# Thirty-five seeded shifts of a planner's priorities and engine preferences, two transformer blocks on one core

## The chip, the cores and the metric

One Trainium2 chip, one of its cores. The metric is the device time of one execution in microseconds (us), here the median of three runs. Each of the core's engines runs its own queue in order: TensorE (PE in the profile), VectorE (DVE), ScalarE (ACT), GpSimd (POOL) and SyncE (SP), the last of which here only issues transfers.

## The reference

A row block of 256 tokens of width 1024 goes through two blocks of two layers each. The first block has adaptive norms (shift, scale and gate from a condition vector), a mixer and a squared-ReLU FFN in each layer; the mixers are a chunked relative-position attention with 16 heads and a gated MLP. The second block has two layers of mixed attention. Everything is float32.

```python
def first_block(x, c, ...):
    cond = jax.nn.silu(c)
    for i in range(DEPTH):
        mod = cond @ ada_w[i] + ada_b[i]
        sh1, sc1, g1, sh2, sc2, g2 = [t[:, None, :] for t in jnp.split(mod, 6, axis=-1)]
        h = rms_norm(x, norm_mix[i]) * (1.0 + sc1) + sh1
        y = chunked_relpos_attention(h, ...) if i == 0 else chunked_spatial_gating(h, ...)
        x = x + g1 * y
        h = rms_norm(x, norm_ffn[i]) * (1.0 + sc2) + sh2
        x = x + g2 * squared_relu_mlp(h, ffn_w1[i], ffn_w2[i])
    return x

def reference(...):
    x = first_block(x, c, ada_w, ada_b, ...)
    return second_block(x, rel_bias_2, pre_norm_g_2, w_in_2, ...)
```

The places that matter here are the entry of the first attention (the projection of `h` to q, k and v), its scores, softmax and out-projection, and the entry of the first FFN.

## The kernel before

The kernel is a program generator. It first records operations (`Op`) in the order of the mathematics, each with its buffers, its dependencies and its alternatives of engine, and then a planner puts them into one order, which is emitted as it stands: each engine executes its instructions in that order. Nothing is reordered on the chip.

**Data.** Tokens lie on partitions in two halves (`t` = 0 and 1). All large weights come from HBM in one list (`wall`), in groups of 1 MB that each hold two tiles of 128x1024, through a ring of four slots named `raw` (`load_group`, issued by SP at L860; a slot is free again when the last reader of both its tiles is done). A weight tile is split into two reduced-precision float32 parts that together carry the precision: `hi` by a cast on ACT (L899) and `lo` by a subtraction on DVE (L903). A product is then a triple of matmuls on PE (L800, L801, L802: hi by hi, hi by lo, lo by hi), with activations split in the same way (L1006 on ACT, L1008 on DVE). Scores and other small products are single matmuls (L788) and transposes are L828. `arena` and `arena_r` are SBUF, `banks` the eight PSUM banks.

**The stretch around the change.** Attention opens with eight steps `k`, each with a weight tile for q and k and one for v, its share of the activations scaled and split, and eight triples. Heads then run in pairs: scores (L788), bias and row minimum (L766 on DVE, 128x256 and 128x128), exponential (L713 on ACT), three transposes of the probabilities (L828) into a PSUM bank, the copy of that bank to SBUF (L728 on ACT, 128x384), and three matmuls with v (L788, 128x64). The scores, the transposes and the results each have a set of banks. The out-projection (weights `ao`) has eight weight tiles and four accumulators. The rows of the condition vector's product (`adc`, L766 on DVE, 128x1024, and `adg`, L758) read their weights from the same ring and are needed for the shift and scale of later norms. After the out-projection come the residual (L739), the sum of squares (L951 on DVE or L949 on ACT), the scaling by the norm (L986 on DVE or L988 on ACT), the transposes, the shift and scale (`affine`, L1064 on DVE or L1070 on ACT, four pieces of 128x128) and the split, and then the first FFN's triples. Its first eight hidden blocks are computed with tokens on partitions and go through a copy (L1359 in `ffn`, executed by the helper at L728 on ACT or L731 on DVE) and four transposes.

**What sets the order.** `Sched.schedule` (L408) plays the program through several times with durations of its own (`round`), derives a due time for each operation and keeps the due times of the best round as priorities `pri`. A last `round` with these priorities gives the order: among the operations that could start about now on an engine, it takes the one with the lowest `pri`. For an operation that may run on ACT or DVE it takes the engine on which start plus duration is least, with 0.6 us added for DVE unless the operation is marked critical:

```python
s, _, e = min(((start_of(o, a[0]), a[1] + (0.0 if o.crit else self.EXTRA.get(a[0], 0.0)), a[0]) for a in o.alts),
        key=lambda x: x[0] + x[1])
```

`shift` can add noise to the priorities of a stretch, but the list of its seeds, `SHIFTS`, is empty.

## Time and profile before

| | |
|---|---|
| time, median of 3 runs | 987.65 us (987.05 to 988.52) |
| the profiled execution's own time | 988.6 us |
| its span | 986.5 us |
| PE busy | 963.1 us (98% of the span) |
| DVE busy | 766.9 us (78%) |
| ACT busy | 616.0 us (62%) |
| HBM read | 214.48 MB, 218 GB/s over the span |

The span is the time from the first to the last instruction; 2.1 us of the execution's own time lie around it. Busy is the time in which an engine executes, waits excluded. The profile lists for each engine what it waited for (the waits), gives the busy time of every engine in chosen stretches together with PEclk, the share of TensorE's full clock of 2.4 GHz that was granted (half of it is 1.2 GHz), and shows single instructions with their start and duration (the timeline). Consecutive instructions of an engine overlap by some 0.1 us in the timeline, so that starts, not durations, show what a sequence costs.

### The profile page before, as it was taken

To read this page: it belongs to the slowest core of one execution; us is meant where nothing else is said; L and a number is where in the kernel's file an instruction comes from. 1 tells how busy PE (TensorE), PEld (TensorE's weight loads), DVE (VectorE), ACT (ScalarE), POOL (GpSimd) and SP (SyncE) were. 2 spreads that over 40 slices of the span, in tenths; PEclk is the share of its full clock that TensorE was granted. 3 is DMA by queue.
4 is the path that set the end of the run, shared out by engine and by line. 5 is a ranking of instruction groups with operands and counts; after the bars stand their busy time and mean duration, and the time that the engine had idled before them with its cause. 6 is when DMAs were issued, how large, how long until landed. Compare 5 with 4: busy or idle time off the path is not lost.

```text
span 986.5 us, 14776 instructions
## 1 busy us (share of the span) xinstructions
PE 963.1 (98%) x5652; PEld 844.5 (86%) x5652; DVE 766.9 (78%) x1300; ACT 616.0 (62%) x1119; POOL 17.2 (2%) x38
## 2 busy tenths in 40 slices
PE   6999899999999999999999999999999999999997
PEld 5878588899998888999999889999889888898986
DVE  6889999978767975987767876765679778898783
ACT  6589857555455666844445764544657689776892
POOL 1000000000100000000000000010000001000000
PEclk7999899999999999999999999999999999999999
DMA  9977676778876594766654375676635126361311
GB/s 348 350 294 293 234 324 255 268 287 306 300 288 235 191 384 171 299 222 239 220 198 146 129 256 217 239 259 224 220 150 211 53 108 228 118 233 68 107 62 44
DMA packets 32087, 216.47 MB, mean 219 GB/s; under 512 B 3793, under 2 KB 4049, under 8 KB 7185
## 3 DMA queue, kind: packets, MB, share of 16 engines
q1 hardware_dynamic: 30816, 211.98, 57.6%
q0 software_dynamic: 1200, 3.56, 1.2%
q8 instruction: 44, 0.72, 0.3%
q14 instruction: 27, 0.21, 0.1%
HBM read 214.48 MB, written 1.05 MB: 218 GB/s over the span
## 4 chain that ended last, share of the span: by engine, by line
PE 87%; ACT 5%; DVE 4%; DMA 2%; issue 1%; SPq 0%; DVEq 0%; ACTq 0%
PE banks L800 26%; PE banks L802 26%; PE banks L801 26%; PE banks L788 4%; PE banks L828 3%; ACT arena L713 2%; DMA raw<-in_wall 1%; ACT arena_r L899 1%; DVE arena L739 1%; ACT arena L728 1%; PE banks L814 1%; PE banks L815 1%; DVE arena L766 1%; DVE arena_r L903 1%; DMA arena<-in_xin 1%
## 5 line engine op out<-in xcount | busy, mean ns | idle before, releaser
L800 PE MATMUL banks<-arena_r 128*128 128x512 f32 (+1 forms) x1568 | 544.1, 347 | 1.3 <-ACT arena_r L1006 0.9
L801 PE MATMUL banks<-arena_r 128*128 128x512 f32 (+1 forms) x1568 | 534.6, 341 | 0.9 <-DVE arena_r L903 0.8
L802 PE MATMUL banks<-arena_r 128*128 128x512 f32 (+1 forms) x1568 | 534.0, 341 | 0.0
L903 DVE TENSOR_TENSOR arena_r<-raw,arena_r 128x1024 fp32r<-128x1024 f32 x300 | 359.7, 1220 | 47.1 <-ACT arena_r L899 46.2
L899 ACT CAST arena_r<-raw 128x1024 fp32r<-128x1024 f32 x300 | 305.7, 1044 | 40.5 <-DMA raw<-in_wall 19.4
L802 PEld LDWEIGHTS banks<-arena_r 128*128 128x128 f32 x1568 | 297.8, 190 | 34.2 <-DVE arena_r L1008 0.2
L800 PEld LDWEIGHTS banks<-arena_r 128*128 128x128 f32 x1568 | 298.3, 190 | 32.0 <-ACT arena_r L1006 1.3
L801 PEld LDWEIGHTS banks<-arena_r 128*128 128x128 f32 x1568 | 298.5, 190 | 31.6 <-DVE arena_r L903 2.1
L713 ACT ACTIVATE arena<-banks 128x256 f32<-128x256 f32 (+1 forms) x100 | 44.0, 443 | 143.9 <-PE banks L802 140.5
L713 ACT ACTIVATE arena<-arena 128x256 f32<-128x256 f32 (+10 forms) x160 | 66.7, 422 | 46.7 <-DVE arena L951 23.0
L1006 ACT ACTIVATE arena_r<-arena 128x256 fp32r<-128x256 f32 (+1 forms) x116 | 54.9, 485 | 63.7 <-DVE arena L758 35.5
L766 DVE CUSTOM_DVE_ANT_0 arena<-raw,arena 128x1024 f32<-128x1024 f32 x64 | 82.0, 1281 | 13.0 <-DMA raw<-in_wall 12.4
L758 DVE SCALAR_TENSOR_TENSOR arena<-banks,arena 128x256 f32<-128x256 f32 (+1 forms) x80 | 37.2, 466 | 51.9 <-ACT arena L713 36.8
L1008 DVE SCALAR_TENSOR_TENSOR arena_r<-arena,arena_r 128x256 fp32r<-128x256 f32 (+1 forms) x116 | 57.4, 504 | 22.8 <-ACT arena_r L1006 22.1
L788 PE MATMUL banks<-arena 128*128 128x64 f32 (+3 forms) x432 | 68.3, 295 | 3.8 <-DMA arena<-in_ident 3.5
L828 PE MATMUL banks<-arena 128*128 128x128 f32 x372 | 58.9, 286 | 11.3 <-ACT arena L728 4.5
L788 PEld LDWEIGHTS banks<-arena 128*128 128x128 f32 x432 | 58.9, 197 | 12.4 <-ACT arena L713 3.7
L828 PEld LDWEIGHTS banks<-arena 128*128 128x128 f32 x372 | 46.7, 148 | 22.8 <-ACT arena L728 6.0
L728 ACT COPY arena<-banks 128x512 f32<-128x512 f32 (+3 forms) x106 | 50.8, 495 | 18.4 <-PE banks L802 9.0
L739 DVE TENSOR_TENSOR arena<-arena 128x512 f32<-128x512 f32 (+6 forms) x128 | 51.6, 431 | 5.0 <-ACT arena L713 1.8
L758 DVE SCALAR_TENSOR_TENSOR arena<-raw,arena 128x1024 f32<-128x1024 f32 x32 | 40.9, 1279 | 5.0 <-DMA raw<-in_wall 4.8
L739 DVE TENSOR_TENSOR arena<-banks,arena 128x512 f32<-128x512 f32 (+1 forms) x48 | 30.0, 641 | 18.0 <-PE banks L802 11.2
(44 smaller groups left out, 381.6 us busy)
## 6 DMA issues: line engine op xcount, KB each, us to landing
raw<-in_wall SPq DMA_DIRECT2D x194, 1024.0 KB, 4.9
raw<-in_wall SPq DMA_DIRECT2D x8, 512.0 KB, 9.1
arena<-in_nbias SPq DMA_DIRECT2D x4, 512.0 KB, 7.3
arena<-in_rows POOLq DMA_DIRECT2D x3, 512.0 KB, 6.6
arena<-in_xin SPq DMA_DIRECT2D x2, 512.0 KB, 4.7
out_dram<-arena SPq DMA_DIRECT2D x4, 256.0 KB, 2.0
arena<-in_dbias POOLq DMA_DIRECT2D x2, 384.0 KB, 3.6
arena<-in_wsT POOLq DMA_DIRECT2D x1, 512.0 KB, 4.6
```

Source lines behind the costliest of these rows:

```text
L713: nc.scalar.activation(out=res(out), in_=res(in_), func=func, scale=res(scale), **kw, **({"accum_out": res(accum)} if accum is not None el ...
L728: alts = [("ACT", (0.05 if psum else 0.093) + n / 1200.0, lambda: nc.scalar.copy(out=res(out), in_=res(in_)))]
L739: alt = ("DVE", 0.068 + n / 960.0, lambda: nc.vector.tensor_tensor(out=res(out), in0=res(a), in1=res(b), op=op))
L758: return self.S.op(("DVE", dur, lambda: nc.vector.scalar_tensor_tensor(out=res(out), in0=res(a), scalar=res(s), in1=res(b), op0=op0, op1=o ...
L766: return self.S.op(("DVE", dur, lambda: nc.vector.tensor_tensor_reduce(out=res(junk if out is None else out), in0=res(a), in1=res(b), scal ...
L788: o = self.S.op(("PE", max(n, 96) * 0.00167, lambda: nc.tensor.matmul(res(out), lhsT=res(l), rhs=res(r), start=start, stop=stop)), rd, [ou ...
L800: nc.tensor.matmul(o, lhsT=lh, rhs=rh, start=start, stop=False)
L801: nc.tensor.matmul(o, lhsT=lh, rhs=rl, start=False, stop=False)
L802: nc.tensor.matmul(o, lhsT=ll, rhs=rh, start=False, stop=stop)
L828: nc.tensor.transpose(res(o), res(i), res(ident))
L899: alts = [("ACT", 0.093 + D / 1200.0, lambda: nc.scalar.copy(out=res(hi), in_=res(src))), ("DVE", 0.068 + D / 1920.0, lambda: nc.vector.te ...
L903: dve = ("DVE", 0.068 + D / 960.0, lambda: nc.vector.tensor_tensor(out=res(lo), in0=res(src), in1=res(hi.f32()), op=ALU.subtract))
```

## The change

The list of seeds gets 35 entries. Each of them picks a stretch of due times, adds normal noise to the priorities of some of the operations there, and now also to a number of each operation, `lean`, that takes the place of the fixed 0.6 us which was added for DVE. The computation, the operations and their dependencies stay the same; what changes is the order on the engines and, for operations with two alternatives, the engine.

```diff
--- before.py
+++ after.py
@@ -314,7 +314,7 @@
 
 
 class Op:
-    __slots__ = ("alts", "pri", "deps", "users", "ndep", "bufs", "table", "ready", "fin", "eng", "extra", "kind", "cnt", "seq", "cyc", "need", "crit", "start", "alt", "tab", "rows")
+    __slots__ = ("alts", "pri", "deps", "users", "ndep", "bufs", "table", "ready", "fin", "eng", "extra", "kind", "cnt", "seq", "cyc", "need", "crit", "start", "alt", "tab", "rows", "lean")
 
 
 LAT_SAME = {"PE": 0.0, "ACT": 0.13, "DVE": 0.13, "POOL": 0.15, "SP": 0.0}
@@ -337,8 +337,10 @@
     HOLD = {"ACT": 0.5, "DVE": 0.5}
     RUSH = 2.0
     WARM = 3300
-    EXTRA = {"DVE": 0.6}
-    SHIFTS = ()
+    SHIFTS = (90566615, 56086312, 43099052, 89024882, 76868707, 18636298, 90523558, 93111676, 38614557,
...
 
     def __init__(self):
         self.ops = []
@@ -358,6 +360,7 @@
         o.users = []
         o.cnt, o.crit = 1, self.crit
         o.cyc, o.rows = (0, 1.0), 128
+        o.lean = 0.0 if self.crit else 0.6
         o.ready, o.fin, o.eng = 0.0, None, None
         deps = set()
         bufs = []
@@ -427,24 +430,29 @@
                 due[o] = t
             for o in self.ops:
                 o.pri = due[o] - (self.RUSH if o.crit else 0.0)
-        pri = list(best[1])
+        order = list(zip(best[1], (o.lean for o in self.ops)))
         for seed in self.SHIFTS:
-            self.shift(best[1], pri, seed)
-        for o, o.pri in zip(self.ops, pri):
+            self.shift(best[1], order, seed)
+        for o, (o.pri, o.lean) in zip(self.ops, order):
             pass
         out = self.round(spaces, slots)
         return [(o, alt, tab, [b.off for b in o.bufs]) for o, alt, tab in out]
 
     @staticmethod
-    def shift(base, pri, seed):
+    def shift(base, order, seed):
 
         rng = np.random.default_rng(seed)
         lo, hi = min(base), max(base)
-        mid, width = rng.uniform(lo, hi), rng.choice([8.0, 20.0, 60.0])
-        size, share = rng.choice([0.7, 2.0, 5.0]), rng.choice([0.1, 0.4, 1.0])
+        mid, width = lo + rng.random() * (hi - lo), rng.choice([6.0, 15.0, 40.0])
+        size, share, turn = rng.choice([0.7, 2.0, 6.0]), rng.choice([0.05, 0.3, 1.0]), rng.choice([0.0, 0.1, 0.5])
         for i, b in enumerate(base):
-            if abs(b - mid) < width and rng.random() < share:
-                pri[i] += size * rng.standard_normal()
+            if abs(b - mid) < width:
+                p, q = order[i]
+                if rng.random() < share:
+                    p += size * rng.standard_normal()
+                if rng.random() < turn:
+                    q += rng.standard_normal()
+                order[i] = p, q
 
     def round(self, spaces, slots):
         for o in self.ops:
@@ -558,7 +566,7 @@
                         _, s, i = min(wait)
                         o = cand[i][1]
                 if len(o.alts) > 1:
-                    s, _, e = min(((start_of(o, a[0]), a[1] + (0.0 if o.crit else self.EXTRA.get(a[0], 0.0)), a[0]) for a in o.alts),
+                    s, _, e = min(((start_of(o, a[0]), a[1] + (o.lean if a[0] == "DVE" else 0.0), a[0]) for a in o.alts),
                             key=lambda x: x[0] + x[1])
                 if best is None or s < best[0]:
                     best = (s, o, e)
```

The order of SP, which issues the loads, stays as it was. 17 operations change their engine, of them 9 at the end of the attention and the entry of the first FFN: two sums of squares go from DVE to ACT, one half of a norm's scaling goes from ACT to DVE and the other back, three shift-and-scale operations change places (two to DVE, one to ACT), and two copies of 128x512 (L1359) go to DVE. Line numbers of the changed kernel are 8 higher (L713 is L721, L899 is L907 and so on).

On PE the order is unchanged up to about 25 us, changed between 25 and 225 us, and nearly unchanged after that. Three places follow; a row is an instruction's line, operation, output, inputs and shape, with xN for N in a row.

ACT towards the end of the scores, before; L713 with inputs in `arena` is the exponential, L899 the cast of an out-projection weight, and the 128x384 copy is that of the transposed probabilities:

```order
L899 CAST arena_r<-raw 128x1024
L713 ACTIVATE arena<-arena 128x256
L713 ACTIVATE arena<-arena 128x128
L713 ACTIVATE arena<-arena 128x256
L899 CAST arena_r<-raw 128x1024
L713 ACTIVATE arena<-arena 128x128
L713 ACTIVATE arena<-arena 128x256
L713 ACTIVATE arena<-arena 128x128
L713 ACTIVATE arena<-arena 128x256
L899 CAST arena_r<-raw 128x1024
L713 ACTIVATE arena<-arena 128x128
L728 COPY arena<-banks 128x384
```

and the changed kernel there:

```order
L736 COPY arena<-banks 128x512
L736 COPY arena<-banks 64x256
L721 ACTIVATE arena<-arena 128x128
L736 COPY arena<-banks 64x256
L736 COPY arena<-banks 128x384
L736 COPY arena<-banks 128x512
L907 CAST arena_r<-raw 128x1024
L736 COPY arena<-banks 128x384
L721 ACTIVATE arena<-arena 128x128
L736 COPY arena<-banks 128x384
L721 ACTIVATE arena<-arena 128x256 x2
L907 CAST arena_r<-raw 128x1024
```

In the first the copy comes behind three casts and eight exponentials; in the second one such copy stands ahead of the first cast and two more ahead of the second.

PE at the same place, before; 128x512 of L788 are scores, L828 transposes, 128x64 the products with v, and L800 to L802 here triples of the out-projection:

```order
L788 MATMUL banks<-arena 128x512
L788 MATMUL banks<-arena 128x256
L800 MATMUL banks<-arena_r 128x512
L801 MATMUL banks<-arena_r 128x512
L802 MATMUL banks<-arena_r 128x512
L800 MATMUL banks<-arena_r 128x512
L801 MATMUL banks<-arena_r 128x512
L802 MATMUL banks<-arena_r 128x512
L828 MATMUL banks<-arena 128x128 x3
L788 MATMUL banks<-arena 128x64
L828 MATMUL banks<-arena 128x128 x9
```

and the changed kernel there:

```order
L796 MATMUL banks<-arena 128x256 x2
L836 MATMUL banks<-arena 128x128 x6
L796 MATMUL banks<-arena 128x512
L796 MATMUL banks<-arena 128x64 x3
L836 MATMUL banks<-arena 128x128 x3
L796 MATMUL banks<-arena 128x64 x6
L808 MATMUL banks<-arena_r 128x512
L809 MATMUL banks<-arena_r 128x512
L810 MATMUL banks<-arena_r 128x512
```

The products with v of three heads now stand ahead of the first out-projection triples, where there was one product behind two triples.

DVE around the last weight of the out-projection and the entry of the first FFN, before; L903 is a weight's second part (first row the out-projection's last, the others the FFN's), L739 the residual, L951 the sum of squares:

```order
L903 TENSOR_TENSOR arena_r<-raw,arena_r 128x1024
L758 SCALAR_TENSOR_TENSOR arena<-arena 128x1
L739 TENSOR_TENSOR arena<-banks,arena 128x512
L739 TENSOR_TENSOR arena<-arena 128x512
L951 ISA arena<-arena 128x512
L951 ISA arena 128x1
L739 TENSOR_TENSOR arena<-banks,arena 128x512
L739 TENSOR_TENSOR arena<-arena 128x512
L951 ISA arena<-arena 128x512
L951 ISA arena 128x1
L749 TENSOR_SCALAR arena<-arena 128x1
L903 TENSOR_TENSOR arena_r<-raw,arena_r 128x1024
```

and the changed kernel there:

```order
L911 TENSOR_TENSOR arena_r<-raw,arena_r 128x1024
L774 ISA arena<-raw,arena 128x1024
L774 ISA arena 128x1
L747 TENSOR_TENSOR arena<-banks,arena 128x512 x2
L747 TENSOR_TENSOR arena<-arena 128x512 x2
L766 SCALAR_TENSOR_TENSOR arena<-arena 128x1
L757 TENSOR_SCALAR arena<-arena 128x1
L911 TENSOR_TENSOR arena_r<-raw,arena_r 128x1024
L994 TENSOR_SCALAR arena<-arena 128x512
L911 TENSOR_TENSOR arena_r<-raw,arena_r 128x1024
L1072 TENSOR_SCALAR arena<-banks,arena 128x128 x4
L911 TENSOR_TENSOR arena_r<-raw,arena_r 128x1024
```

The pass L774 of 128x1024 (L766 before) came from some thirty operations further up to behind the last out-projection weight, the two sums of squares have left the engine, both halves' residuals now stand together, and an affine (L1072) has come to the engine.

## Rows read from the trace of the kernel before

**Rows 1.** The page, part 1: busy time, share of the span and instructions:
```profile
PE 963.1 (98%) x5652; PEld 844.5 (86%) x5652; DVE 766.9 (78%) x1300; ACT 616.0 (62%) x1119; POOL 17.2 (2%) x38
```
**Rows 2.** PE's waits: engine, line, waited for: us in total, times, longest:
```profile
PE banks L828 <- ACT arena L728: 4.5, 3, 3.1
...
PE banks L828 <- DVE arena L739: 1.4, 2, 1.2
...
PE banks L801 <- DVE arena_r L903: 0.8, 1, 0.8
```
**Rows 3.** Stretch: length, busy PE, PEld, DVE, ACT, POOL, PEclk, DMA share, GB/s:
```profile
75.00:100.00 25.00, 24.97 (x146) 20.40 (x145) 24.45 (x66) 22.45 (x62) 2.00 (x4) 1.00 0.71 274
100.00:125.00 25.00, 20.55 (x91) 14.46 (x90) 24.31 (x68) 20.68 (x60) 0.00 (x0) 0.86 0.68 257
```
**Rows 4.** The same view of shorter stretches:
```profile
67.75:71.55 3.80, 2.29 (x12) 1.30 (x11) 3.77 (x7) 3.41 (x8) 0.00 (x0) 1.00 0.00 0
82.90:137.73 54.83, 50.35 (x281) 40.21 (x280) 53.12 (x129) 42.99 (x106) 2.00 (x4) 0.94 0.72 285
111.90:118.40 6.50, 2.29 (x8) 1.05 (x6) 6.46 (x15) 6.50 (x21) 0.00 (x0) 0.85 0.38 147
118.40:123.30 4.90, 4.88 (x20) 4.14 (x21) 4.87 (x14) 3.68 (x7) 0.00 (x0) 0.50 0.88 318
...
174.90:178.00 3.10, 1.80 (x16) 1.60 (x16) 3.10 (x4) 3.10 (x4) 0.00 (x0) 1.00 0.82 344
```
**Rows 5.** Timeline of PE, 107 to 119 us: start, us, instruction, idle before:
```profile
107.34 0.49 PE L828 MATMUL banks<-arena 128*128 128x128 f32 x3
...
118.42 0.90 PE L828 MATMUL banks<-arena 128*128 128x128 f32 x3 [3.08 <-ACT arena L728]
```
**Rows 6.** Timeline of ACT, 116 to 118 us:
```profile
116.58 1.03 ACT L899 CAST arena_r<-raw 128x1024 fp32r<-128x1024 f32 x1
...
117.91 1.93 ACT L728 COPY arena<-banks 128x384 f32<-128x384 f32 x4
```
**Rows 7.** Timeline of DVE, 48 to 55 us:
```profile
50.24 0.42 DVE L1008 SCALAR_TENSOR_TENSOR arena_r<-arena,arena_r 128x256 fp32r<-128x256 f32 x1
50.98 1.23 DVE L903 TENSOR_TENSOR arena_r<-raw,arena_r 128x1024 fp32r<-128x1024 f32 x1 [0.33 <-ACT arena_r L899]
52.13 1.28 DVE L766 CUSTOM_DVE_ANT_0 arena<-raw,arena 128x1024 f32<-128x1024 f32 x1
```
**Rows 8.** Timeline of DVE, 116 to 150 us:
```profile
116.10 1.28 DVE L766 CUSTOM_DVE_ANT_0 arena<-raw,arena 128x1024 f32<-128x1024 f32 x1
...
136.59 1.22 DVE L903 TENSOR_TENSOR arena_r<-raw,arena_r 128x1024 fp32r<-128x1024 f32 x1
...
141.65 0.69 DVE L739 TENSOR_TENSOR arena<-banks,arena 128x512 f32<-128x512 f32 x1
...
148.35 1.29 DVE L1008 SCALAR_TENSOR_TENSOR arena_r<-arena,arena_r 128x512 fp32r<-128x512 f32 x2 [0.39 <-ACT arena_r L1006]
```
**Rows 9.** Timeline of PE, 145 to 151 us:
```profile
145.51 1.03 PE L828 MATMUL banks<-arena 128*128 128x128 f32 x8
146.30 0.48 PE L800 MATMUL banks<-arena_r 128*128 128x512 f32 x1
...
150.50 0.39 PE L800 MATMUL banks<-arena_r 128*128 128x512 f32 x1
```
**Rows 10.** Timeline of ACT, 146 to 149 us:
```profile
146.15 1.50 ACT L1070 ACTIVATE arena<-banks,arena 128x128 f32<-128x128 f32 x4
147.68 1.16 ACT L1006 ACTIVATE arena_r<-arena 128x512 fp32r<-128x512 f32 x2
```
**Rows 11.** Timeline of ACT, at 176.6 us:
```profile
176.61 0.58 ACT L728 COPY arena<-banks 128x512 f32<-128x512 f32 x1
```
**Rows 12.** Groups by line and shape, of DVE: busy us, mean ns:
```profile
L731 DVE COPY arena<-banks 128x512 f32<-128x512 f32 x4 | 2.7, 684 | 0.1
```
**Rows 13.** The page, part 6: issues, KB each, us to landing:
```profile
raw<-in_wall SPq DMA_DIRECT2D x194, 1024.0 KB, 4.9
```

3 lines of the change are left out of this document (added).

## The prediction

> **What bounds the kernel now.** I read part 1 of the page first: PE is busy for 963.1 us, 98% of the span [rows 1], so all that an order can win back is the 23.4 us in which PE stands, and what those waits cost afterwards. PE's waits come next [rows 2]: besides the start and the end, the largest item is transposes (L828) that wait for the copy L728, 4.5 us in three waits, and 1.4 us behind L739. The busy times by stretch say where: PE is full from 75 to 100 us, and from 100 to 125 us it is busy for only 20.55 of 25 us at a mean granted clock of 0.86 [rows 3]. In the same 25 us DVE is busy for 24.31, and between 75 and 100 us for 24.45. So two engines take turns here: DVE has no air, and PE has a hole.
>
> The hole in detail. Between 111.90 and 118.40 us PE works 2.29 of 6.50 us, so it stands 4.21 us; right behind it, from 118.40 to 123.30, it is busy for 4.88 us at clock 0.50, 1.2 GHz [rows 4], which at full clock would be 2.44 us of work. One wait of 3.08 us ends at 118.42 with the copy L728 [rows 5]. That copy starts at 117.91, right behind a cast L899 of 1.03 us [rows 6], though the transposes that it copies started at 107.34 [rows 5]: it was ready some ten microseconds earlier, and ACT did casts and exponentials meanwhile (the rows of ACT's order before show which). The rest are two smaller holes: 1.51 us between 67.75 and 71.55, and 1.30 us between 174.90 and 178.00 [rows 4].
>
> **The trace on the clock.** A wait costs its length and, here, 2.44 us more in the 4.9 us behind it [rows 4]. The Trainium skill, "TensorE: Matmul & The Clock Gate", section "What's actually happening", says that the slow clock is the default state and that activity releases it, so by its rule every long hole is paid twice. The trace agrees at 118 us and bounds the rule from the other side: holes of 1.51 us and of 1.30 us went with clock 1.00 [rows 4]. Were the wait that I expect below at the FFN's entry (1.6 us) to halve the clock, the sum would be 2.4 us worse; by the two rows I take nothing for it.
>
> **Part 1, the opening (16 to 75 us).** At step k = 6 ACT now casts the v weight ahead of splitting the activations, and DVE runs that weight's L903 and one L766 ahead of the split L1008. By starts, the L903 to L766 step takes 1.15 us and the L766 some 1.3 [rows 7]. So the split, at 50.24 us before, is over at about 53.5 us, while PE's first triple of that step stands at 51.2 and can run two of its three matmuls without it: a new wait of 1.9 us. It mostly replaces one: PE waits 1.51 us at 67.75 [rows 4] for norms on DVE, so arriving 1.9 us later there it finds them done, and DVE's own chain is not longer. Net between 0.4 us lost and 0.4 won; I take 0. If DVE's chain were held up too, all 1.9 us would be lost: the upper bound.
>
> **Part 2, heads and out-projection (75 to 138 us).** The copy goes ahead of the casts and PE gets three heads' products before the first out-projection triple (rows of ACT's and PE's order). So the hole and its slow clock go, 4.21 + 2.44 = 6.65 us of PE. What is late next is DVE, which makes the out-projection's second parts. Its last L903 starts at 136.59 and the next thing on DVE at 137.73. From 82.90 to 137.73 DVE is busy for 53.12 of 54.83 us, idle 1.71 [rows 4]. The order puts one L766 pass, 1.28 us, which ran at 116.10 [rows 8], behind that last L903. The others ahead of it are the same operations. Without any idle time the L903 ends at 137.73 - 1.28 - 1.71 = 134.7 us; I leave half of the idle time in, 135.5.
>
> PE then has two triples for token half 0, 0.7 us each (six in 4.2 us between 146.30 and 150.50 [rows 9]), until about 137; the pass of 1.28 us and the first half's residual step occupy DVE until 137.5. The second residual started at 141.65 [rows 8], and the half's transposes at 145.51 [rows 9], 3.9 us later. The sums of squares move to ACT, which is idle there; two residual steps now lie in a row, which is about even with that. Transposes: 137.5 + 3.9 = 141.4 us, 4.1 us earlier.
>
> **Part 3, the entry of the first FFN.** Before, six triples (4.2 us) stood between the transposes and the FFN's first triple at 150.50 [rows 9] and covered shift, scale and split. Now two do, since the other four have moved ahead. The chain is: first four transposes 0.6, affine 1.4 (1.50 on ACT [rows 10]; on DVE now), one L903 of 1.15 that DVE has in between, one split of 0.65 (two L1008 in 1.29 [rows 8]): 141.4 + 3.8 = about 145.3 us. PE's work ends at 141.4 + 0.8 + 1.4 = 143.6, so a wait of 1.6 to 1.7 us appears that was not there. The first FFN triple comes at 145.3 in place of 150.50: **5.2 us won**, of the 6.65.
>
> **Part 4, inside the FFN (150 to 225 us).** The copy at 176.61 us stands behind casts on ACT [rows 11] and made the 1.30 us hole [rows 4]. It goes to DVE (0.684 us there [rows 12] against 0.58), and four more triples of 128x256 (1.4 us) stand ahead of its transposes. So 1.3 us won. Against it: PE now runs 5 us earlier against the same loads and casts, and by the same running sums three second parts come 0.2 to 0.4 us late, and other small ones; I take 1.2 us back. Behind that weights lie many microseconds ahead of their use, and from 225 us the order is nearly the same, so I carry the gain to the end.
>
> **The sum.** 0 + 5.2 + 1.3 - 1.2 = 5.3 us. Against the profiled execution's 988.6 us this is 983.3; the median of the runs lies 0.95 us lower, so **982.4 us**. All the holes named and the slow clock together are 1.51 + 4.21 + 2.44 + 1.30 = 9.5 us; that is the bound of the gain: 978.1.
>
> **Rivals.**
>
> *Almost all of it comes through (978 to 980 us).* If the affine chain is covered, as by triples that come later than I think, the 1.6 us at the FFN's entry and the 1.2 us behind it are kept: 8.1 us, 979.5. For it: PE's order has moved only four triples. Against it: the running sums leave that wait even with no idle time on DVE.
>
> *DVE takes it back (same, 985.7 to 988).* DVE is busier than PE from 100 to 125 us [rows 3], and the change does not lighten it up to the FFN: the postponed L766 (1.28) only moves behind the last L903, where the residual waits for it, and two copies of 0.684 us and an affine come to DVE. If the 1.71 us of idle time stay too (they were waits for ACT and loads, not for PE), the last L903 comes only 1.28 us earlier, the pass then costs it again, and what is left is part 4 and some tenths: about 0.5 to 1.5 us, 986.6. The Trainium skill, "Perfetto Trace Analysis", section "Identifying the Most-Contended Engine", says to improve the engine with the highest occupancy in the regime; by that rule, too, a change of ACT's order would win little here. The trace agrees on the occupancies. What speaks against it: PE's hole came from neither load nor DVE, and DVE's waits in this stretch were mostly for ACT.
>
> *Slower: a ring slot held too long (about 990 us).* The postponed L766 reads a tile of the ring and holds one of four slots until 136 us in place of 117. A load takes 4.9 us from issue to landing [rows 13], and SP issues strictly in order, so a late slot delays all weights behind it. If one out-projection or FFN weight comes a landing late, PE stands 4.9 us; long enough, as at 118 us, to lose another 2.44 us to the clock: 7.3 us lost against 5.3 won, 989.7. It decides from the point at which the three other slots no longer keep up with PE, one group for each two weights. For it: between 111.90 and 118.40 us the DMA share is 0.38 [rows 4], that is, loads did stop for want of a slot. Against it: casts move earlier on ACT, and with them the release of the other three.
>
> **How the numbers follow.** A gain of 3 to 7 us as worked out: 0.50. Almost all: 0.20. DVE takes it back: 0.18. Slot or another new wait: 0.12. About 0.2%, 2 us, is what can be told from no change here. Both gains are faster than 985.7: faster 0.70; same 0.18; slower 0.12. The range goes from the bound of the gain, 978, through all of the case "same" on its lower side to 988.5, and leaves out the slower case and a little beside.
>
> **What would show it.** Right: PE busy over 24 of 25 us between 100 and 125 us with PEclk 1.00; no wait of L828 for L728 above 1 us; the last out-projection L903 ending by 136 us; the first FFN triple at 145 to 146 us behind a wait of 1 to 2 us; from there to the end the same length as before. Wrong: a wait of PE for L903 or for a load between 110 and 145 us; a clock of 0.50 anywhere past the opening; a first FFN triple after 148 us; or a stretch behind 225 us that is longer by over 1 us.

## The result, and the profile after

| | before | changed kernel |
|---|---|---|
| time, median of 7 runs each | 987.65 us (986.98 to 989.93) | 981.89 us (979.82 to 985.62) |
| the profiled execution, its span | 988.6, 986.5 us | 983.17, 981.1 us |

The ratio is 0.9938 with a 95% interval of 0.9924 to 0.9952: 5.8 us faster, where 5.3 was forecast. Lines of the file are 8 higher now: L728 is L736, L766 is L774, L828 is L836, L800 to L802 are L808 to L810, L903 is L911.

The page of the changed kernel, part 1, beside [rows 1]: the engines do what they did; the span is shorter by 5.4 us.

```profile
PE 960.7 (98%) x5652; PEld 841.9 (86%) x5652; DVE 766.6 (78%) x1302; ACT 614.8 (63%) x1117; POOL 17.3 (2%) x38
```

PE's waits in the changed kernel, beside [rows 2] (us in total, times, longest). The transposes' wait for the copy, 4.5 us, is gone from the list. L808 and L810, which wait for the split of the activations, now stand high; of their 4.1 us, 2.0 lie in the opening (1.76 of them one wait at 52.21 us), 1.2 at 16.27 us, where the kernel before has 0.9, and 0.92 at the entry of the first FFN.

```profile
PE banks L836 <- ACT arena L996: 4.6, 1, 4.6
...
PE banks L808 <- ACT arena_r L1014: 2.1, 3, 1.2
PE banks L810 <- DVE arena_r L1016: 2.0, 2, 1.8
```

The stretches of [rows 3] and the one behind them, changed kernel (length, busy PE, PEld, DVE, ACT, POOL, PEclk, DMA share, GB/s). PE works 24.51 us from 100 to 125 us where it worked 20.55, at clock 1.00 where it had 0.86; DVE is as full as it was up to 125 us and fuller behind.

```profile
75.00:100.00 25.00, 24.74 (x144) 20.03 (x143) 24.34 (x66) 23.43 (x64) 0.62 (x2) 1.00 0.71 271
100.00:125.00 25.00, 24.51 (x134) 18.68 (x132) 24.27 (x72) 20.93 (x62) 1.46 (x2) 1.00 0.76 278
125.00:150.00 25.00, 24.08 (x123) 19.62 (x122) 24.78 (x40) 17.37 (x28) 0.00 (x0) 1.00 0.82 312
```

The last of these stretches in the kernel before:

```profile
125.00:150.00 25.00, 25.00 (x143) 21.64 (x142) 22.22 (x42) 14.04 (x21) 0.00 (x0) 1.00 0.79 321
```

Timeline of DVE in the changed kernel around the end of the out-projection (start, us, instruction, idle before), beside [rows 8]: the last second part now starts at 134.70 instead of 136.59, the postponed pass stands behind it, then both residuals.

```profile
134.70 1.22 DVE L911 TENSOR_TENSOR arena_r<-raw,arena_r 128x1024 fp32r<-128x1024 f32 x1
135.83 1.28 DVE L774 CUSTOM_DVE_ANT_0 arena<-raw,arena 128x1024 f32<-128x1024 f32 x1
...
137.19 1.38 DVE L747 TENSOR_TENSOR arena<-banks,arena 128x512 f32<-128x512 f32 x2
```

Timeline of PE there, beside [rows 9]: transposes at 141.82 (145.51 before), and the first FFN triple, in three rows with two waits, from 145.03 (150.50 before).

```profile
141.82 1.09 PE L836 MATMUL banks<-arena 128*128 128x128 f32 x8
...
145.03 0.50 PE L808 MATMUL banks<-arena_r 128*128 128x512 f32 x1 [0.72 <-ACT arena_r L1014]
145.37 0.40 PE L809 MATMUL banks<-arena_r 128*128 128x512 f32 x1
145.96 0.50 PE L810 MATMUL banks<-arena_r 128*128 128x512 f32 x1 [0.20 <-DVE arena_r L1016]
```

**The lead.** Executions come to the end of the heads at different times. PE's matmul number 453 is a product of scores; ahead of it every kernel here has done the same work on PE, if in another order. It starts between 105.09 us (e11) and 108.49 us (e9), though the PE orders of these two are the same up to there. So the table below counts from that matmul: by how many us each kernel's profiled execution is then ahead of the profiled execution of before, at the same place of PE's order. It is worked out from starts in the traces, one execution for each kernel; the columns are named by the time in before, and the first gives the start of matmul 453 itself (106.91 us in before).

```
                   matmul   out-proj.  first FFN  FFN      FFN
                   453 at   144 us     150.5 us   168 us   199 us   end
changed kernel     106.85    6.42       5.41       4.85     5.70     5.36
e1_heads           108.01    6.56       0.87       0.95     2.37     1.82
e2_heads_ffn       106.42    6.55       5.54       5.01     5.88     4.86
e3_open_ffn        107.92   -0.11      -0.99      -1.33    -0.05    -1.43
e4_copies          107.10   -0.40      -0.40      -0.45     1.06     0.88
e5_heads_tr        107.30    6.54       4.49       2.37     2.75    -0.66
e6_tr_back         107.41    6.52       2.33       2.52     2.24     1.96
e7_turns           105.65    6.53       4.63       1.51     2.59     2.72
e8_entry           107.73    6.52       6.17       4.37     5.19     5.39
e9_pass_ahead      108.49    5.20       4.19       3.65     4.39     4.53
e10_pool           106.81    5.80       4.79       4.22     3.00     3.08
e11_copies_act     105.09    4.82       2.24       1.68     0.48    -0.07
e12_light          105.23    6.53       4.56       4.01     5.41     5.47
```

The column at 144 us holds the whole idea of the change: with the new order of the heads a kernel is 6.4 to 6.6 us ahead at the end of the out-projection. (e9 and e10 change DVE's work there; e11 has the same order, but its execution came early and then waited at 118 and 122 us.) The column at 150.5 us decides what becomes of the lead.

### The profile page after: what moved, and what is told of

Its sections match the earlier page's. It is cut to its first block, busy times and chain, and to the rows that moved or that the text cites. A ratio compares the mean times of both kernels' runs of the same rounds, so it can differ in the third digit from the quotient of the medians.

```text
span 981.1 us, 14771 instructions
## 1 busy us (share of the span) xinstructions
PE 960.7 (98%) x5652; PEld 841.9 (86%) x5652; DVE 766.6 (78%) x1302; ACT 614.8 (63%) x1117; POOL 17.3 (2%) x38
## 4 chain that ended last, share of the span: by engine, by line
PE 82%; DVE 6%; DMA 4%; ACT 4%; issue 2%; SPq 0%; DVEq 0%; ACTq 0%
PE banks L808 24%; PE banks L810 24%; PE banks L809 24%; PE banks L796 5%; DMA raw<-in_wall 4%; PE banks L836 3%; DVE arena_r L911 2%; DVE arena L774 2%; ACT arena_r L907 1%; PE banks L822 1%; ACT arena L721 1%; PE banks L823 1%; DVE arena L766 1%; ACT L1694 1%; DMA arena<-in_xin 1%
## 5 line engine op out<-in xcount | busy, mean ns | idle before, releaser
L808 PE MATMUL banks<-arena_r 128*128 128x512 f32 (+1 forms) x1568 | 544.9, 348 | 2.9 <-ACT arena_r L1014 2.1
L810 PE MATMUL banks<-arena_r 128*128 128x512 f32 (+1 forms) x1568 | 534.2, 341 | 2.0 <-DVE arena_r L1016 2.0
L911 DVE TENSOR_TENSOR arena_r<-raw,arena_r 128x1024 fp32r<-128x1024 f32 x300 | 360.2, 1221 | 48.5 <-ACT arena_r L907 45.2
L907 ACT CAST arena_r<-raw 128x1024 fp32r<-128x1024 f32 x300 | 305.3, 1043 | 67.3 <-PE banks L810 38.2
L810 PEld LDWEIGHTS banks<-arena_r 128*128 128x128 f32 x1568 | 297.5, 190 | 37.2 <-DVE arena_r L1016 3.3
L808 PEld LDWEIGHTS banks<-arena_r 128*128 128x128 f32 x1568 | 297.9, 190 | 35.4 <-ACT arena_r L1014 3.2
L721 ACT ACTIVATE arena<-banks 128x256 f32<-128x256 f32 (+1 forms) x100 | 44.1, 443 | 115.2 <-PE banks L810 108.0
L774 DVE CUSTOM_DVE_ANT_0 arena<-raw,arena 128x1024 f32<-128x1024 f32 x64 | 81.9, 1280 | 20.5 <-DMA raw<-in_wall 20.2
L721 ACT ACTIVATE arena<-arena 128x256 f32<-128x256 f32 (+10 forms) x160 | 66.7, 422 | 13.7 <-DVE arena L774 5.0
L766 DVE SCALAR_TENSOR_TENSOR arena<-banks,arena 128x256 f32<-128x256 f32 (+1 forms) x80 | 37.2, 466 | 32.0 <-PE banks L796 17.0
L836 PE MATMUL banks<-arena 128*128 128x128 f32 x372 | 56.6, 278 | 5.6 <-ACT arena L996 4.6
L736 ACT COPY arena<-banks 128x512 f32<-128x512 f32 (+3 forms) x103 | 49.6, 492 | 17.2 <-PE banks L810 7.8
L836 PEld LDWEIGHTS banks<-arena 128*128 128x128 f32 x372 | 45.9, 145 | 16.8 <-ACT arena L996 5.5
L766 DVE SCALAR_TENSOR_TENSOR arena<-raw,arena 128x1024 f32<-128x1024 f32 x32 | 41.1, 1283 | 10.8 <-DMA raw<-in_wall 10.7
```

The lines of the kernel that those rows point to most:

```text
L721: nc.scalar.activation(out=res(out), in_=res(in_), func=func, scale=res(scale), **kw, **({"accum_out": res(accum)} if accum is not None el ...
L766: return self.S.op(("DVE", dur, lambda: nc.vector.scalar_tensor_tensor(out=res(out), in0=res(a), scalar=res(s), in1=res(b), op0=op0, op1=o ...
L774: return self.S.op(("DVE", dur, lambda: nc.vector.tensor_tensor_reduce(out=res(junk if out is None else out), in0=res(a), in1=res(b), scal ...
L808: nc.tensor.matmul(o, lhsT=lh, rhs=rh, start=start, stop=False)
L810: nc.tensor.matmul(o, lhsT=ll, rhs=rh, start=False, stop=stop)
L836: nc.tensor.transpose(res(o), res(i), res(ident))
```

## Experiments

Each kernel below executes an order that is put together from the two known ones, engine by engine: `b` is the order of before, `a` the changed one. `put(b, a, ALL, parts)` takes the named parts of `a` into `b`, on all engines: 0 is the opening up to some 72 us, 1 the heads and the out-projection, 2 everything behind, with the entry of the FFN. `move(q, op, to, engine)` puts one operation ahead of another, on another engine if one is named. The excerpts show only the lines that build the order, with comments added; `ALL` stands for the five engines. Line numbers of these kernels are 69 to 73 higher than the changed kernel's (its L808 is L877 to L881). The medians of before beside them were 987.89, 988.65 and 988.76 us. My theory was the prediction's: the hole at 112 to 123 us is what is won, DVE is next, the entry of the FFN takes a part back. The rival was that another part wins it, or that DVE takes it back.

### Which part of the order wins

**e1_heads**: part 1 alone.

```diff
-        return a
+        return put(b, a, ALL, (1,))
```

> Heads and out-projection (about 72 to 138 us) in the changed order, everything ahead of and behind them in the order of before. Theory (the gain is the hole in PE at 112 to 123 us, and the opening is neutral): the hole and its slow clock are gone, token half 0's transposes come at about 141.5 us, six triples follow them as before, so the first FFN triple stands at about 146.5 in place of 150.5, and the hole at 177 us stays: 983.6 us, 4.0 won. Rival (DVE takes it back): the out-projection's last second part still sets the end, not under 986.3. Rival (the opening or the FFN's engine turns bring most): not under 985.5.

Measured 987.25 us (985.67 to 989.75), ratio 0.9992 (0.9981 to 1.0003): nothing. The expectation failed, though the hole at 118 us was gone and the lead at 144 us was the full 6.56 us. Timeline of PE in e1_heads at the entry of the FFN:

```profile
139.82 0.39 PE L879 MATMUL banks<-arena_r 128*128 128x512 f32 x1
144.09 1.09 PE L905 MATMUL banks<-arena 128*128 128x128 f32 x8 [3.88 <-ACT arena L1065]
```

Its stretches there:

```profile
139.82:144.10 4.28, 0.41 (x3) 0.02 (x1) 4.21 (x10) 2.33 (x5) 0.00 (x0) 1.00 0.92 366
144.10:148.50 4.40, 4.40 (x18) 3.60 (x19) 3.24 (x8) 3.69 (x8) 0.00 (x0) 0.65 0.47 164
```

The hole has moved: PE comes 6.5 us early to transposes that need the residual, its sum of squares and its scaling, stands 3.88 us, and works at a mean clock of 0.65 behind it. The first FFN triple comes at 150.73, as in before.

**e2_heads_ffn**: parts 1 and 2, that is, the changed kernel with the opening of before.

```diff
-        return a
+        return put(b, a, ALL, (1, 2))
```

> The changed kernel with the opening (up to about 72 us) in the order of before. Theory: PE's new wait at step k = 6 is absorbed by the wait for the norms, so the opening is neutral: 981.9 us within 0.5, the same as the changed kernel. Rival (the new wait and its slow clock, some 3 us in the changed trace, cost time at the end): 979 to 980. Rival (the opening's order brings part of the gain): 983 to 984.

Measured 983.46 us (981.60 to 985.26), ratio 0.9954 (0.9936 to 0.9972). So parts 1 and 2 together bring most of the gain. The time lies in the range of the rival that gives the opening a part of it, but the intervals overlap: what the opening is worth in the median, between nothing and some 1.6 us, was not settled. (The lead says nothing of it, since it counts from a point behind the opening.)

**e3_open_ffn**: the changed kernel with part 1 of before.

```diff
-        return a
+        return put(a, b, ALL, (1,))
```

> The changed kernel with heads and out-projection (about 72 to 138 us) in the order of before; the engine turns at the FFN's entry are in. Theory: the hole at 112 to 123 us is back; the FFN's entry has two triples as cover in place of six, which costs 1.5 us when PE has no lead, and 1.3 us come back at 177 us: 987.9 us (987.2 to 988.7). Rival (the engine turns or the opening bring the gain themselves): not over 985.5.

Measured 990.41 us, ratio 1.0020 (1.0008 to 1.0033): a little slower than before, by more than expected. The hole is back (PE waits 3.08 us for L805, the copy, at 119.45), and the new order of the entry, without a lead to use, costs 1.2 us between 144 and 168 us.

**e4_copies**: before, with only the two copies moved ahead of the cast on ACT that stood before them.

```diff
-        return b
+        for i in (487, 496):
+            b = move(b, i, 592)   # 592: a cast of the out-projection's first weight
+        return b
```

> The kernel before, with two of ACT's operations moved and nothing else: the copies of the transposed probabilities of heads 8 and 9 go ahead of the first cast of an out-projection weight. Theory: the wait of 3 us at 118 us and the slow clock behind it go, the first out-projection triples come 0.9 us later, and then DVE's order, which is that of before, sets the end: 1 to 2.5 us won, about 985.9 us. Rival (that copy's place on ACT is the whole cause): 4 to 5 us won, 982.7 to 983.7. Rival (DVE sets the whole stretch): 987.6, nothing won.

Measured 989.54 us (987.02 to 992.99), ratio 1.0021 (1.0006 to 1.0035). This small repair of the line that the waits named won nothing. Timeline of PE in e4_copies:

```profile
116.62 0.50 PE L907 MATMUL banks<-arena 128*128 128x128 f32 x3
119.84 1.36 PE L907 MATMUL banks<-arena 128*128 128x128 f32 x6 [2.72 <-ACT arena L807]
```

And of ACT:

```profile
117.51 1.04 ACT L978 CAST arena_r<-raw 128x1024 fp32r<-128x1024 f32 x1
...
118.84 1.32 ACT L807 COPY arena<-banks 128x512 f32<-128x512 f32 x3
```

The same wait is there one copy further down the chain, behind the next cast. Of the orders tried, only that of the whole part (e1) takes the wait away; which of its moves are needed beside the copies was not tried.

### What keeps the lead at the entry of the FFN

**e5_heads_tr**: e1 and, from the changed order, PE's alone: the half's eight transposes (677, 681) and one triple go behind four triples of the out-projection.

```diff
         b = put(b, a, ALL, (1,))
+        for i in (666, 677, 681):
+            b = move(b, i, 662)   # 662: a triple of the out-projection
         return b
```

> The kernel of e1_heads (heads and out-projection in the changed order, the rest of before) with three kinds of PE's operations moved and nothing else: the eight transposes of token half 0 at the FFN's entry go behind four triples of the out-projection that stood behind them, as they stand in the changed kernel. Engines and all else at the entry stay as before. Theory now (the hole only moved to the transposes, where PE stood for 3.9 us and then ran on a slow clock; what turns the lead into time is PE's order at the entry): the wait at the transposes is under 1 us, one of 1 to 2 us appears at the first FFN triple, clock 1.00, first FFN triple 3 to 4 us earlier than before: 984.3 us. Rival (the engine turns shorten the chain and are what the gain needs): 986 or more.

Measured 988.88 us, ratio 1.0002 (0.9993 to 1.0010). The triples do cover the chain: 4.49 us of lead at the first FFN triple instead of 0.87. But then it is waited away piece by piece: 1.13 us for DVE at 152.39, 0.93 for the copy on ACT at 174.89, and the rest far behind, most of it at 344, 727, 853 and 934 us. The expectation (984.3 us) failed. Timeline of PE in e5_heads_tr:

```profile
152.39 0.50 PE L881 MATMUL banks<-arena_r 128*128 128x512 f32 x1 [1.13 <-DVE arena L829]
...
174.89 0.66 PE L908 MATMUL banks<-arena 128*128 128x128 f32 x4 [0.93 <-ACT arena L808]
```

**e6_tr_back**: the reverse; the changed kernel with the transposes ahead of those triples.

```diff
+        for i in (677, 681):
+            a = move(a, i, 657)   # 657: the first of the four triples
         return a
```

> The changed kernel with one move: the eight transposes of token half 0 at the FFN's entry go ahead of four triples of the out-projection, as before; engines as in the changed kernel. Theory: PE waits some 2.7 us at the transposes and runs on a slow clock behind them, and the first FFN triple comes 1.2 (no slow clock) to 2.7 us (slow clock) later than in the changed kernel: 984.0 us. Rival (the engine turns at the entry bring the gain, not the cover): within 0.5 us of the changed kernel, 982.4 or less.

Measured 985.39 us (982.71 to 987.14), ratio 0.9965 (0.9953 to 0.9978). Timeline of PE in e6_tr_back:

```profile
142.26 1.97 PE L907 MATMUL banks<-arena 128*128 128x128 f32 x8 [2.62 <-DVE arena L1065]
```

Its stretch right behind that wait:

```profile
142.30:144.90 2.60, 2.60 (x11) 2.41 (x12) 2.52 (x6) 1.71 (x4) 0.00 (x0) 0.50 0.75 208
```

The wait and the lower clock, 0.50 or 1.2 GHz, cost 3.1 us of lead against the changed kernel. So the place of eight transposes is worth some 3 us, given the lead, more than the 2.1 us expected.

**e7_turns**: the changed kernel with the turns and engines of this half's residual, sums of squares, scaling and shift as before.

```diff
+        for i, to, e in ((645, 646, None), (638, 645, "DVE"), (647, 590, "DVE"), (652, 695, "DVE"),
+                         (651, 703, "ACT"), (678, 682, "ACT"), (682, 704, "DVE")):
+            a = move(a, i, to, e)
         return a
```

> The changed kernel with the engines of token half 0's entry into the FFN as before (both sums of squares on DVE, the two halves of the norm's scaling and the two shift-and-scale operations exchanged); PE's order as changed. Theory (DVE has no air between 125 and 150 us, so each operation that comes back to it delays the chain): the transposes come about 1 us later, the first FFN triple 1.0 to 1.5 us later than in the changed kernel, and it stays so: 983.2 us. Rival (only the order counts, the engine turns are worth nothing): 981.9, the first FFN triple at the same time counted from 107 us.

Measured 984.79 us (983.52 to 987.03), ratio 0.9962 (0.9949 to 0.9975). Timeline of PE in e7_turns:

```profile
141.61 1.09 PE L908 MATMUL banks<-arena 128*128 128x128 f32 x8 [1.01 <-ACT arena L1068]
...
144.61 0.50 PE L880 MATMUL banks<-arena_r 128*128 128x512 f32 x1 [0.51 <-ACT arena_r L1086]
144.94 0.40 PE L881 MATMUL banks<-arena_r 128*128 128x512 f32 x1
146.66 0.50 PE L882 MATMUL banks<-arena_r 128*128 128x512 f32 x1 [1.32 <-DVE arena_r L1088]
```

Its stretch behind them:

```profile
146.66:150.20 3.54, 3.54 (x10) 2.77 (x11) 3.54 (x7) 2.87 (x5) 0.00 (x0) 0.60 0.30 125
```

Three waits in place of one of 0.72 and one of 0.20, and a slow clock: 3.3 us of lead lost within five triples (4.63 to 1.31), of which 1.4 came back by the end. This is more than twice what was expected, and the fallen clock is part of it. The share of ACT and DVE in the entry matters nearly as much as PE's order: 2.6 us of lead at the end, where e6 lost 3.4.

**e8_entry**: the changed kernel with eleven more moves by hand at the entry, the postponed pass behind the residual among them, so that the split is ready when PE comes.

```diff
+        for i, to, e in ((676, 589, None), (589, 695, None), (590, 695, None), (651, 695, None),
+                         (680, 704, None), (678, 679, "ACT"), (682, 683, None), (644, 656, None),
+                         (635, 644, None), (677, 666, None), (681, 666, None)):
+            a = move(a, i, to, e)
         return a
```

> The changed kernel with eleven operations at the FFN's entry moved by hand: one more L766 pass goes behind the last out-projection L903, the postponed one goes behind the residual, PE's last two triples of token half 0 go one triple earlier and the transposes two triples earlier, shift and scale of the first group run on ACT, and the first splits go ahead of a weight's second part. Theory (DVE's L903 sets the out-projection, and the chain behind it sets the first FFN triple): the last L903 ends at about 134.7 us in place of 135.9, the waits at the first FFN triple (1.26 us) go, and that triple comes 1.2 us earlier: 980.8 us. Rival (PE's own work sets the entry, or a load waits for the slot that the postponed pass holds): 981.9 or more.

Measured 984.04 us (983.75 to 985.31), ratio 0.9957 (0.9946 to 0.9969): the waits at the first FFN triple are gone and the lead there is 6.17 us, but what was pushed back on DVE is waited for a few triples later, and at the end the lead is the changed kernel's. The expectation of 980.8 us failed. Timeline of PE in e8_entry:

```profile
145.87 0.50 PE L883 MATMUL banks<-arena_r 128*128 128x512 f32 x1
...
150.87 0.50 PE L882 MATMUL banks<-arena_r 128*128 128x512 f32 x1 [0.84 <-DVE arena L830]
```

The profile names L830; the weight's second part just ahead of it on DVE, which this hi-by-lo product needs, ends at 150.81 us.

### What comes next in the out-projection

**e9_pass_ahead**: the changed kernel with the postponed pass at its old place, among the second parts.

```diff
+        a = move(a, 589, 609)   # the pass, ahead of the third second part
         return a
```

> The changed kernel with one DVE operation moved back: the postponed L766 pass of 1.2 us stands ahead of the out-projection's third L903 again. Theory (DVE's running sum sets the out-projection): all later L903 come 1.2 us later, the last ends at about 137.1 us, PE waits that much more, and the first FFN triple comes 0.8 to 1.2 us later: 982.9 us. Rival (PE sets the out-projection and DVE has slack): 981.9, and no new wait.

Measured 985.53 us (981.87 to 986.81), ratio 0.9960 (0.9945 to 0.9976). Timeline of PE in e9_pass_ahead:

```profile
123.26 0.50 PE L878 MATMUL banks<-arena_r 128*128 128x512 f32 x1 [0.94 <-DVE arena_r L980]
```

Timeline of DVE:

```profile
137.67 1.22 DVE L980 TENSOR_TENSOR arena_r<-raw,arena_r 128x1024 fp32r<-128x1024 f32 x1
```

A pass of 1.28 us more ahead of the second parts makes PE wait for one of them, and 1.2 us of lead are gone (5.20 in place of 6.42); by the end it is 0.8. DVE has no air there. The rest of the 2.4 us between this execution and the changed kernel's is not the pass: it came to matmul 453 1.6 us later. Two of the six runs took 981.87 and 981.96 us.

**e10_pool**: the changed kernel with two second parts on POOL.

```diff
+        a = move(a, 624, 628, "POOL")   # sixth weight of the out-projection
+        a = move(a, 704, 682, "POOL")   # a weight of the first FFN
         return a
```

> The changed kernel with two of DVE's subtractions of 128x1024 (the second parts of the out-projection's sixth weight and of the FFN's third) done by POOL, which has nothing else to do there; no run here shows what one costs on POOL. Theory (DVE is what bounds the stretch up to the FFN): the last out-projection L903 ends some 1.15 us earlier and the first FFN triple comes 0.5 to 1.2 us earlier: 981.0 us. Rival (PE sets the pace by now, or POOL's work holds up DVE's): 982 or more.

Measured 983.38 us (981.31 to 985.62), ratio 0.9941 (0.9926 to 0.9956): no gain. Timeline of POOL in e10_pool:

```profile
128.24 2.78 POOL L987 TENSOR_TENSOR arena_r<-raw,arena_r 128x1024 fp32r<-128x1024 f32 x1 [12.43 <-ACT arena_r L980]
```

Timeline of DVE in the same microseconds:

```profile
129.66 0.76 DVE L820 TENSOR_TENSOR arena<-banks,arena 128x256 f32<-128x256 f32 x2 [0.88 <-PE banks L869]
130.34 1.76 DVE L847 CUSTOM_DVE_ANT_0 arena<-raw,arena 128x1024 f32<-128x1024 f32 x1
```

POOL takes 2.78 us for what DVE does in 1.22, PE waits 0.46 us for it, and DVE stands idle for 0.88 us until PE's products come, with the pass that overlaps POOL's end at 1.76 us instead of 1.28. The relief of one engine became a wait for the other.

**e12_light**: the changed kernel in its own order, with three passes of DVE over 64 columns instead of 1,024, so that it leaves out part of the sums of that row. In the excerpt `bias` stands for a longer expression, and the helper's new parameter is left out.

```diff
-            self.ttr(None, src, self.condb.v(), D, bias, ALU.mult, ALU.add, c)
+            n = 64 if (l, m) == (0, 3) and k >= 5 else D
+            self.ttr(None, src[:, 0:n], self.condb.v()[:, 0:n], D, bias, ALU.mult, ALU.add, c, n)
```

> The changed kernel in its own order; only the last three passes of DVE over the modulation's shift row 3 run over 64 of their 1,024 columns, so that DVE has three times about 1.2 us = 3.6 us less to do between 127 and 135 us, and PE the same as ever. (It leaves out part of the sums that make this row, so it computes something else than the reference.) Theory (DVE's full turn sets the out-projection and the entry): the last second part of the out-projection ends at least 2 us earlier than the 135.9 us of the changed kernel, counted from the same product of the heads, and the waits of 1.26 us at the first FFN triple shrink below 0.5; the first FFN triple starts some 1 to 1.5 us earlier; the end keeps most of that, median 980.5 to 981.5 us. Rival (the chain through ACT and the loads set the entry, DVE is only busy beside it): the waits at the first FFN triple stay above 1 us and the time stays at 981.9 within 0.3. Second rival (lead is given back to whatever is tight next): the wait goes, the lead at 145 us is there, and less than half of it is left by 200 us.

Measured 981.77 us (980.59 to 983.43), ratio 0.9937 (0.9921 to 0.9954). My theory fell here: DVE is 3 us lighter, and PE is not earlier. Timeline of DVE in e12_light:

```profile
131.22 0.28 DVE L843 CUSTOM_DVE_ANT_0 arena<-raw,arena 128x64 f32<-128x64 f32 x1
...
132.04 1.23 DVE L981 TENSOR_TENSOR arena_r<-raw,arena_r 128x1024 fp32r<-128x1024 f32 x1 [0.53 <-ACT arena_r L977]
...
135.46 1.37 DVE L816 TENSOR_TENSOR arena<-banks,arena 128x512 f32<-128x512 f32 x2 [0.99 <-PE banks L879]
```

Timeline of ACT:

```profile
136.52 2.01 ACT L977 CAST arena_r<-raw 128x1024 fp32r<-128x1024 f32 x2 [4.52 <-DMA raw<-in_wall]
138.43 0.62 ACT L1027 ACTIVATE arena<-arena 128x512 f32<-128x512 f32 x1
```

Timeline of PE:

```profile
141.04 1.10 PE L905 MATMUL banks<-arena 128*128 128x128 f32 x8 [0.87 <-DVE arena L1064]
...
144.25 0.51 PE L877 MATMUL banks<-arena_r 128*128 128x512 f32 x1 [0.72 <-ACT arena_r L1084]
```

The last second part starts at 132.04, counted from matmul 453 1.0 us earlier than in the changed kernel (26.81 against 27.85), not 2 or more, because the cast ahead of it is now late. The residual then waits 0.99 us for PE's own triples: PE is full up to 139.8 us. And the sum of squares stands on ACT behind two casts that wait 4.52 us for a load, which costs the transposes 0.87 us. This last wait is not DVE's doing: the load was issued 0.6 us earlier than in the changed kernel, counted from the same matmul, and took 8.7 us to land where it took 5.2 there; why stays open. Without it PE would have won little all the same: the residual, from which the chain to the transposes starts, is only 0.1 us earlier than in the changed kernel. So in the changed kernel three things lie within about a microsecond of each other at the end of the out-projection: PE's triples, DVE's second parts, and the loads. More work on DVE shows at once (e9), less does not, in the median either.

### The copies inside the FFN

**e11_copies_act**: the changed kernel with the two copies of 128x512 back on ACT.

```diff
+        a = move(a, 756, 815, "ACT")
+        a = move(a, 770, 746, "ACT")
         return a
```

> The changed kernel with the two copies of 128x512 inside the FFN back on ACT, in their places of before. Theory now (the hole of 1.3 us at 177 us belonged to that one execution, since e1_heads and e4_copies ran through the same order there without it): no wait of PE above 0.5 us between 165 and 185 us, 981.9 us within 0.5. Rival (the prediction's term, the copy late on ACT): a wait of about 1.3 us, 983.2 us.

Measured 982.62 us (980.78 to 986.63), ratio 0.9943 (0.9925 to 0.9962): not to be told from the changed kernel. Its profiled execution, the slowest of its runs, has the waits. Timeline of PE in e11_copies_act:

```profile
170.10 0.66 PE L906 MATMUL banks<-arena 128*128 128x128 f32 x4 [0.48 <-ACT arena L806]
...
176.55 0.66 PE L906 MATMUL banks<-arena 128*128 128x128 f32 x4 [1.58 <-ACT arena L806]
```

Against my expectation of no wait above 0.5 us, the copies on ACT do make PE stand 2.1 us. But e1 and e4, with before's order in this place, do not show the hole at 177 us that before shows; by the lead table they are 1.4 to 1.5 us better than before between 168 and 199 us. e5, with the copies on ACT too, has 0.93 us of it (at 174.89). So this hole comes in some executions and not in others, and what moving the copies is worth in the median was not settled.

## Why the prediction was right, and where its steps were off

**Opening, taken as 0: right for the profiled execution, and partly by luck.** The new wait came, 1.76 us where 1.9 was expected (the rows of the prediction's own sum put the end of the split at 53.1 us and not at 53.5, so that some 1.5 us follow from them). And the wait for the norms went: of the 1.51 us at 67.75 us [rows 4] nothing is left. One assumption in the prediction failed: that a wait of this length costs no clock. Two stretches of the changed kernel, the wait and what follows:

```profile
50.00:52.20 2.20, 0.46 (x2) 0.02 (x1) 2.20 (x5) 0.49 (x1) 0.00 (x0) 1.00 1.00 333
52.20:56.00 3.80, 3.79 (x10) 3.02 (x11) 3.29 (x6) 3.06 (x5) 0.00 (x0) 0.55 1.02 427
```

From 48.9 to 55.7 us the changed kernel's execution lost 4.1 us on that of before, and at 71 us, by the start of the heads, the two were 0.1 us apart all the same. 2.4 us came back, most of it where before waits for the norms. The rest was a head start that the changed order did not make: the profiled execution of before ran the first triples at half clock, that of the changed kernel did not.

Before:

```profile
16.20:20.90 4.70, 4.66 (x11) 3.65 (x12) 4.66 (x9) 2.81 (x5) 0.00 (x0) 0.50 1.03 428
```

Changed kernel:

```profile
16.20:20.90 4.70, 4.60 (x19) 3.52 (x20) 4.66 (x9) 3.63 (x6) 0.00 (x0) 1.00 1.04 429
```

The fair pair is e2, with before's opening and full clock at the start: it is 2.9 us ahead of the changed kernel at PE's matmul 187, and 0.1 us at matmul 259 (71.12 us), behind its waits for the norms. So in this pair the wait for the norms did swallow the new wait and its clock. But in e12, with the changed opening and the same start, the wait at 52.22 us was 1.24 us, the clock stayed at 1.00, and matmul 259 came at 69.60 us, 1.5 us ahead of both. So in these executions the opening costs nothing where the clock falls and wins 1.5 us where it does not; how often it falls over many runs was not measured. Timeline of PE in e12_light there:

```profile
52.22 0.49 PE L879 MATMUL banks<-arena_r 128*128 128x512 f32 x1 [1.24 <-DVE arena_r L1086]
```

And its stretch behind that wait:

```profile
52.20:56.00 3.80, 3.78 (x17) 3.15 (x18) 3.28 (x6) 2.97 (x5) 0.00 (x0) 1.00 1.03 425
```

**Heads and out-projection: right in mechanism and size.** Forecast: 6.65 us of PE come free, the last second part ends at 135.5, transposes at 141.4. Measured: 6.4 to 6.6 us of lead in seven of the eight kernels that have the changed heads as they are (e11's execution has 4.82), an end at 135.92, transposes at 141.82. "What is late next is DVE" holds in one direction only: e9 shows that more work on DVE delays PE, e12 that less does not bring it forward.

**The entry of the FFN: right in size, wrong in the story.** Forecast: 5.2 us kept, behind a new wait of 1.6 to 1.7 us. Measured: 5.41 us kept, a wait of 0.72 and one of 0.20 us that delay PE by 1.26 together. The prediction spoke of the four triples that moved ahead of the transposes as cover that was lost. The runs show them to be the cover that keeps the gain: with the old entry (e1) 5.7 of the 6.56 us are gone at the first FFN triple. Likewise the new share of ACT and DVE, which the prediction booked as about even, is worth some 3 us there (e7). (DVE had one of the two shift-and-scale groups of this half before, too, L1064 at 146.59 us; the engines exchanged theirs.) And the clock, which it took as safe at this place, stayed at 1.00 in the changed kernel but fell in e1, e6 and e7.

**Inside the FFN: +1.3 and -1.2, of which the sum held.** From the first FFN triple to 168 us the changed kernel lost 0.56 us, by 199 us it had won back 0.85. So 0.3 us were won in all where +1.3 and -1.2 gave 0.1: the sum held, and both terms were too large. The +1.3 hangs on a hole that before, e5 and e11 have and e1 and e4, with the copies on ACT too, have not; what it comes to in the median is open.

**From 225 us on "the same length": right**, within 0.4 us (5.7 to 5.36). The single executions of e3 and e5 lost 1.4 and 3.4 us behind 225 us, e5 most of it at 344, 727, 853 and 934 us; why stays open.

**The rivals.** "Almost all comes through" failed at the entry's wait; e8 shows that taking that wait away only moves it to 150.87 us. "DVE takes it back" did not happen to the change as a whole, but e1 is that case with another cause: not DVE's load but the chain from residual to transposes without cover. The late ring slot did not come: PE has no wait for a weight, its cast or its second part in the changed kernel. The loads are near, though; with DVE lighter it is a load that holds up the cast ahead of the last second part (e12).

## What to carry to other kernels

A wait that is taken away on a full engine gives a lead, and a lead is only worth what the next dependence chain leaves of it: 6.5 us of lead gave 0.9 us at the next stage with the old order there, and 5.4 us with work of the earlier stage kept back to stand ahead of that chain and the chain shared anew between two engines. So move both places together, and follow the lead from operation to operation between two traces instead of counting waits. Moving the one instruction that a wait names (e4), or the work of a busy engine to a free one (e10), won nothing here.

## What the runs showed of the hardware that I had not expected

- The length of a wait alone doesn't tell whether PE's clock falls. Standing times of 1.30 and 1.51 us [rows 4] and waits of 1.49 and 1.58 us (e11, at 143.24 and 176.55) went on at 1.00, and so did the opening's wait where it was 0.54 us (e7) or 1.24 (e12). Where it was 1.75 or 1.76, in the changed kernel and in e3, e6, e8, e9 and e10, half clock followed, in the changed kernel 0.55 over 3.8 us. In e7 a wait of 1.32, the third within some 6 us, was followed by 0.60 over 3.5 us; 2.62 us (e6) by 0.50 over 2.6, 3.88 us (e1) by 0.65 over 4.4.
- A subtraction of 128x1024 took 2.78 us on POOL (2.38 the second time) against 1.22 on DVE, and a pass of DVE that overlapped it 1.76 instead of 1.28 us (e10; the stretched pass was seen once).
- A pass over 64 columns took 0.28 us against 1.28 for 1,024 (e12). If the time grows evenly with the columns, 0.2 us or so are paid whatever the width; this is an estimate from the two.
- Much of the difference between executions goes with the clock in the opening. Among the eight with the changed opening and heads, the five with half clock behind the opening's wait started matmul 453 at 106.81 to 108.49 us, the three without (e7, e11, e12) at 105.09 to 105.65. Coming early is not always kept: e12 kept it, while e11 came 1.8 us earlier than the changed kernel and ended 3.7 us later.
